# Hybrid decoder trunk on one core: VectorE merges the plain and the shared sums of a block pair, and an order is fixed between one step's last low part and the next step's first difference

## The chip, the cores and the metric

The kernel runs on one core of a Trainium2 chip. The metric is the device time of one execution in microseconds (us), given as the median of several runs. Beside it stands one profiled execution of the kernel, whose trace the views below come from. The engines are TensorE (PE in the views, with PEld for its weight loads), VectorE (DVE), ScalarE (ACT), GpSimd (POOL) and SyncE (SP); SP and POOL issue the transfers.

## The reference

One layer of a decoder trunk over 272 rows (16 meta tokens and 256 tokens) of 2048 float32 numbers: a combined projection, retention heads beside mLSTM heads, an output projection, and then a gated feed-forward part. Only the last part bears on the change:

```python
u = rmsnorm(h, norm_ffn)
up = causal_dwconv(u @ w_up, ffn_conv_w, ffn_conv_b)
gate, val = jnp.split(up, [FFN_DIM], axis=-1)          # FFN_DIM = 5632
h = h + (jax.nn.silu(gate) * val) @ w_down             # (256, 5632) @ (5632, 2048)
...
h = rmsnorm(h, norm_final)                             # meta rows are dropped
```

## The kernel before

**Numbers in two parts.** All products run in a 32-bit form of TensorE with fewer bits than float32. So each operand is split into a high part (a cast by ScalarE, tiles `whi`) and a low part (operand minus high part, by VectorE, tiles `wlo`), and three products are summed: high by high, high by low, low by high. For weights of a plain step this is `load_w` (lines 113 to 122): SP loads `wraw` (line 116), ScalarE casts (119), VectorE subtracts (121). `wraw` has four buffers, `whi` and `wlo` five each.

**Stages.** Input projection and heads, output projection (`in_wo`), then the feed-forward part in two halves of 22 tiles of 128 hidden columns each: in each half the up projection (`in_wu`), the convolution and the gate, and then the down projection (`in_wd`). The trace has the down projection of the first half from about 718 to 831 us, that of the second half from about 1083 to 1196 us.

**The down projection.** The output is 256 rows (two row tiles, `tt`) by 2048 columns (four blocks of 512, `b`). It is worked through in two pairs of blocks, `b` = 0 and then `b` = 2 (line 915). Each pair has 11 steps `q` over pairs of hidden tiles. Steps 0, 4, 9 and 10 are plain: four direct products (two row tiles, two blocks), into four PSUM banks `cs[tt, j]` (tiles `atps`, line 828). Steps 1, 2, 3, 5, 6, 7 and 8 are fast (`FAST`, function `seven`): the 2x2 block product is made with seven products instead of eight. Three of the seven go straight into the banks `cs`; the other four go into four shared banks `ps` (tiles `mmps`), whose sums and differences are wanted by several blocks. The last pair of the second half (`final`) takes the steps in another order, with two of the fast ones done plainly.

**A fast step** (`seven`, lines 830 to 869): SP loads the four weight tiles into one of two homes `left[turn]` (tile `hT`, lines 838 and 839; the first of them was made earlier and kept in DRAM). VectorE makes three differences of them: two at once into `ta` (line 842) and one into `tb` (line 843), which are buffers of `wraw`. Four groups are then split in turn by ScalarE and VectorE (lines 764 and 766): two from `hT`, then `ta`, then `tb`. TensorE takes the high parts (857, 858) and the low parts (860). A buffer of `wraw` comes free for SP's next load when the low part made from it is done.

**The end of a pair** (the border). After the last fast step, `share` (lines 878 to 894) empties the four shared banks: ScalarE copies `p1` into `x1` (882), VectorE makes `x6`, `x7`, the second `x6` and `x5` (884, 885, 887, 893), and each of the four is added onto its block of the result `hn` by an accumulating transfer of POOL (`onto`, line 876). After the last plain step the four banks `cs` are copied by ScalarE (line 949) into `x` tiles, and each is added onto its block by another accumulating transfer. A block thus gets two accumulating transfers at a border. There are three such borders: after the pairs 0 and 2 of the first half and after pair 0 of the second; the final pair is finished by VectorE in line 898. The first split of the next pair is placed behind the last copy of the border (`emptied`, line 854).

**What sets the order.** Each engine takes its own queue strictly in order. The order within a queue is chosen when the kernel is built, from the program's order and an estimate of when each instruction could run; `tc.issue_after(ins)` puts the instructions in its block behind `ins` where they are on the engine of `ins`. It makes no wait between engines.

Of the kernel before, what the change touches and what calls it, by code (L numbers as in the profile page):

```python
# [10 lines left out]
F32 = mybir.dt.float32  # L11
F32R = mybir.dt.float32r
AF = mybir.ActivationFunctionType
ALU = mybir.AluOpType
PSUM = bass.MemoryType.PSUM

P = 128
# [66 lines left out]
def trunk(ctx: ExitStack, tc: tile.TileContext, io, out: bass.AP):  # L84
    nc = tc.nc
# [120 lines left out]
    with pool("sq", 1, side="right") as sqp:  # L206
        for k0, k1 in [(0, 1), (1, 2)] + [(k, k + 2) for k in range(2, KT, 2)]:
            n = k1 - k0
# [3 lines left out]
            raw = wpool.tile([P, 2, W0], F32, name="wraw", bufs=4)[:, :n, :]  # L212
# [5 lines left out]
            for k in range(k0, k1):  # L218
                nc.scalar.activation(xh[:, k, :], hT[:, k, :], AF.Copy, scale=pcol("gmix", k))
                nc.vector.scalar_tensor_tensor(out=xl[:, k, :], in0=hT[:, k, :], scalar=pcol("gmix", k),  # L220
                                               in1=xh[:, k, :].bitcast(F32), op0=ALU.mult, op1=ALU.subtract)

            hi = wpool.tile([P, 2, W0 + GW], F32R, name="whi", bufs=5)[:, :n, :]
            lo = wpool.tile([P, 2, 2 * P], F32R, name="wlo", bufs=5)[:, :n, :]
            for i in ((slice(0, 1), slice(1, 2)) if k0 == 2 else (slice(0, n),)):
                copied = nc.scalar.copy(hi[:, i, 0:W0], raw[:, i])
                nc.vector.tensor_tensor(out=lo[:, i], in0=raw[:, i, 0 : 2 * P], in1=hi[:, i, 0 : 2 * P].bitcast(F32), op=ALU.subtract)
                parted = nc.vector.tensor_tensor(out=hi[:, i, W0:], in0=raw[:, i, 2 * P :], in1=hi[:, i, 2 * P : W0].bitcast(F32), op=ALU.subtract)
            for k in range(k0, k1):
                i = k - k0  # L230
                first, last = k == 0, k == KT - 1
                for j, (ps, t0) in enumerate(((k_ps, 0), (q_ps, TQ))):
                    w = hi[:, :, j * P : (j + 1) * P], lo[:, :, j * P : (j + 1) * P]
# [428 lines left out]
    midp_cm = pool("midp", 1, side="left")  # L662
    midp = midp_cm.__enter__()
    ss4 = midp.tile([P, 2, 5], F32, name="ss4")
    x5 = midp.tile([P, 5, 512], F32, name="x5")
    pace = midp.tile([P, 1], F32, name="pace")

    def x_tile(i):
        return x5[:, i, :]
# [74 lines left out]
    for half in range(2):  # L744
# [18 lines left out]
        def split(hi, lo, x, after=None):  # L763
            copied = nc.scalar.copy(hi, x)  # L764
            with tc.issue_after(after.ins) if after else nullcontext():
                return copied, nc.vector.tensor_tensor(out=lo, in0=x, in1=hi.bitcast(F32), op=ALU.subtract)  # L766
# [44 lines left out]
        if half == 1:  # L811
            table("natural_log_exp_and_others", copied)

        def product(ps, tt, q, w, first=False, last=False, c0=0, n0=0, n1=6, seed=False, seeded=False):

            hi, lo = w
            rows = slice(tt * P, (tt + 1) * P)
            cols = slice(c0, c0 + ps.shape[1])
            if q in PLAIN:
                k = 2 * PLAIN.index(q)  # L820
                ah, al = ([m[:, k + i, rows] for i in range(2)] for m in (mh, ml))
            else:
                f = FAST.index(q)
                ah, al = ([m[:, f, A12 if i else A11, :] if tt == 0 else m[:, f, A22, :] if i else a[:, BOTH.index(q), :] for i in range(2)]
                          for m, a in zip((sh, sl), a21))
            parts = [(a[i], hi, i) for i in range(2) for a in (ah, al)] + [(ah[i], lo, i) for i in range(2)]
            for n, (a, m, i) in list(enumerate(parts))[n0:n1]:
                nc.tensor.matmul(ps, a, m[:, i, cols], start=first and n == 0, stop=seed or last and n == 5, skip_group_check=seeded)  # L828

        def seven(b, q, cs, ps, first, last, after, norm):  # L830


            nonlocal turn
            f = FAST.index(q)
            raw = left[turn]
            turn = 1 - turn

            nc.sync.dma_start(raw[:, 0, :], early[b, q])
            nc.sync.dma_start(raw[:, 1:4, :], io["wd7"][b // 2, half * NQD + q][:, 1:4, :])
            ta, tb = (wpool.tile([P, 2, 512], F32, name="wraw", bufs=4) for _ in range(2))  # L840

            nc.vector.tensor_tensor(out=ta, in0=raw[:, 0:1, :].to_broadcast([P, 2, 512]), in1=raw[:, 1:3, :], op=ALU.subtract)
            nc.vector.tensor_tensor(out=tb[:, 0, :], in0=raw[:, 3, :], in1=raw[:, 0, :], op=ALU.subtract)
            copied = None
            for w, to in (
                (raw[:, 2:4, :], ((S4, cs[0, 1], False, False), (A12, cs[0, 0], False, False))),
                (raw[:, 0:2, :], ((S2, ps[2], first, last), (A11, ps[0], first, last))),
                (ta, ((S3, ps[1], first, last), (S1, ps[3], first, last))),
                (tb[:, 0:1, :], ((A22, cs[1, 0], False, False),)),
            ):  # L850
                hi = wpool.tile([P, 2, 512], F32R, name="whi", bufs=5)
                lo = wpool.tile([P, 2, 512], F32R, name="wlo", bufs=5)
                n = len(to)
                with tc.issue_after(after.ins) if first and after else nullcontext():
                    copied, _ = split(hi[:, :n, :], lo[:, :n, :], w)
                for i, (m, o, begin, _) in enumerate(to):
                    nc.tensor.matmul(o, sh[:, f, m, :], hi[:, i, :], start=begin, stop=False)  # L857
                    nc.tensor.matmul(o, sl[:, f, m, :], hi[:, i, :], start=False, stop=False)  # L858
                for i, (m, o, _, end) in enumerate(to):
                    nc.tensor.matmul(o, sh[:, f, m, :], lo[:, i, :], start=False, stop=end)  # L860
            if norm:

                with tc.issue_after(copied.ins):
                    for g in norm:
                        squares(*g)
                reached = nc.gpsimd.tensor_tensor(out=junk[:, 0:1], in0=tb[:, 0, 0:1], in1=tb[:, 0, 0:1], op=ALU.add)
                with tc.issue_after(reached.ins):
                    for tt, _, c0, c1 in norm:
                        times_gain(tt, c0, c1)
# [4 lines left out]
        def onto(tt, b, x):  # L874

            nc.gpsimd.dma_start(block(tt, b), x, accum_op=ALU.add)  # L876

        def share(ps, b, final):

            p1, p7, p6, p5 = ps  # L880
            x6, x7, x5, x1 = (x_tile(i) for i in range(4))
            nc.scalar.copy(x1, p1)  # L882
            onto(0, b, x1)
            nc.vector.tensor_tensor(out=x6, in0=p6, in1=x1, op=ALU.add)
            nc.vector.tensor_tensor(out=x7, in0=p7, in1=x6, op=ALU.add)
            onto(1, b, x7)
            nc.vector.tensor_tensor(out=x6, in0=x6, in1=p5, op=ALU.subtract)
            if final:

                nc.vector.tensor_tensor(out=block(0, b + 1), in0=block(0, b + 1), in1=x6, op=ALU.add)  # L890
            else:
                onto(0, b + 1, x6)
            nc.vector.tensor_tensor(out=x5, in0=x7, in1=p5, op=ALU.subtract)
            onto(1, b + 1, x5)

        def add(ps, tt, c0):
            h = hn[:, tt, c0 : c0 + ps.shape[1]]
# [17 lines left out]
        for b in (0, 2):  # L915
            cs = {}
            for j in range(2):
                for tt in range(2):
                    cs[tt, j] = at.tile([P, 512], F32, name="atps")
            ps = [mm.tile([P, 512], F32, name="mmps") for _ in range(4)]  # L920

            final = half == 1 and b == 2
            steps = [0, 1, 4, 2, 7, 3, 5, 6, 8, 9, 10] if final else range(NQD)
            fast = [q for q in steps if q in FAST and not (final and q in BOTH)]
            plain = [q for q in steps if q not in fast]
            alone = plain[-lag:] if final else []
            for q in steps:
                if q in fast:
                    due = []
                    if final and q != fast[0]:  # L930
                        due, gains = gains[:1], gains[1:]
                    seven(b, q, cs, ps, q == fast[0], q == fast[-1], emptied, due)
                    if q == fast[-1]:
                        with tc.high_priority() if final else nullcontext():
                            share(ps, b, final)
                    continue
                for j in range(2):
                    if j == 1 and q in alone:
                        continue
                    w = load_step(b + j, q)  # L940
                    for tt in range(2):
                        product(cs[tt, j], tt, q, w, q == plain[0], q == plain[-1 - (lag if final and (tt, j) == (1, 1) else 0)])
            for j in range(2):
                for n, tt in enumerate(range(2)):
                    c = (b + j) * 512
                    if not final:

                        x = x_tile((4, 3, 1, 0)[2 * j + n])
                        emptied = nc.scalar.copy(x, cs[tt, j])
                        onto(tt, b + j, x)  # L950
                        if half == 1:
                            gains.append((tt, b + j, c, c + 512))
                    elif j == 0:
                        add(cs[tt, j], tt, c)
                        squares(tt, b, c, c + 512)
                        times_gain(tt, c, c + 512)
# [116 lines left out]
```

## Time and profile before

| | us |
|---|---|
| median of 3 runs (lowest to highest) | 1206.83 (1206.01 to 1209.47) |
| the profiled execution's own time | 1206.01 |
| its span in the trace | 1204.2 |
| TensorE busy | 1194.5 |
| VectorE busy | 971.1 |
| ScalarE busy | 708.1 |
| GpSimd busy | 167.3 |

The rest of the profiled execution's time, 1.8 us, lies around the span. Busy time is a sum over the whole span; an engine that is busy for less than the span can still be the one that others wait for in one stage. The transfers of the program move 263.27 MB.

### The profile page before, as it was taken

How to read it: one execution, taken by the hardware profiler on the slowest of the kernel's cores; microseconds unless marked ns; L12 is line 12 of the kernel's file. 1: busy time of each engine (PE TensorE's matmuls, PEld its weight loads, DVE VectorE, ACT ScalarE, POOL GpSimd, SP SyncE). 2: the span in 40 equal slices, each digit the busy share in tenths (PEclk: the TensorE clock that was granted, in tenths of full speed). 3: DMA queues.
4: the chain of work that ended last, by engine and by line, in shares of the span. 5: the costliest groups of instructions: out<-in, count | busy, mean ns of one | idle time of the engine just before them, and what ended most of it. 6: DMA issues, size and time to landing. Idle time of an engine off the chain costs nothing.

```text
span 1204.2 us, 22798 instructions
## 1 busy us (share of the span) xinstructions
PE 1194.5 (99%) x8956; PEld 1151.2 (96%) x8956; DVE 971.1 (81%) x1446; ACT 708.1 (59%) x964; POOL 167.3 (14%) x222
## 2 busy tenths in 40 slices
PE   9999999999999999999999999999999999999997
PEld 9999999999999999999999998878999999998886
DVE  8967778766775966788888889997697878789897
ACT  8747746655656656555555556665554655556664
POOL 0100001111110311021112100202023112100232
PEclk9999999999999999999999999999999999999999
DMA  8865565566565965766866744949777767755956
GB/s 280 275 208 162 169 187 169 197 182 192 171 189 168 345 204 176 252 219 203 263 217 212 225 178 175 272 182 272 279 249 250 234 247 242 253 184 211 281 170 200
DMA packets 83005, 263.27 MB, mean 219 GB/s; under 512 B 14673, under 2 KB 18897, under 8 KB 82769
## 3 DMA queue, kind: packets, MB, share of 16 engines
q1 hardware_dynamic: 71952, 223.85, 56.9%
q0 software_dynamic: 10368, 37.11, 10.1%
q8 instruction: 70, 1.15, 0.4%
q10 hardware_dynamic: 576, 0.85, 0.2%
q14 instruction: 39, 0.31, 0.1%
HBM read 243.42 MB, written 11.27 MB: 211 GB/s over the span
## 4 chain that ended last, share of the span: by engine, by line
PE 97%; DMA 1%; DVE 1%; ACT 0%; issue 0%; SPq 0%; DVEq 0%; ACTq 0%
PE mmps L128 26%; PE mmps L129 25%; PE mmps L131 25%; PE atps L828 8%; PE mmps L860 2%; PE mmps L857 2%; PE mmps L858 2%; PE atps L858 1%; PE atps L857 1%; PE atps L860 1%; PE atps L380 1%; DMA wraw<-in_wd 1%; PE atps L372 0%; DMA hT<-in_xT 0%; PE atps L128 0%; PE atps L131 0%
## 5 line engine op out<-in xcount | busy, mean ns | idle before, releaser
L119 ACT CAST whi<-wraw 128x1024 fp32r<-128x1024 f32 x352 | 368.5, 1049 | 311.0 <-PE mmps L129 200.9
L121 DVE TENSOR_TENSOR wlo<-wraw,whi 128x1024 fp32r<-128x1024 f32 x352 | 432.5, 1231 | 68.9 <-ACT whi L119 66.7
L128 PE MATMUL mmps<-uh,whi 128*128 128x258 f32 x1408 | 346.1, 283 | 0.0
L129 PE MATMUL mmps<-ul,whi 128*128 128x258 f32 x1408 | 346.0, 283 | 0.0
L128 PEld LDWEIGHTS mmps<-uh,whi 128*128 128x128 f32 x1408 | 267.6, 190 | 0.1
L129 PEld LDWEIGHTS mmps<-ul,whi 128*128 128x128 f32 x1408 | 267.1, 190 | 0.1
L128 PE MATMUL mmps<-xh,whi 128*128 128x272 f32 (+2 forms) x864 | 219.8, 288 | 0.0
L129 PE MATMUL mmps<-xl,whi 128*128 128x272 f32 (+2 forms) x864 | 218.3, 286 | 0.0
L131 PE MATMUL mmps<-uh,wlo 128*128 128x258 f32 x1408 | 196.5, 282 | 0.0
L131 PEld LDWEIGHTS mmps<-uh,wlo 128*128 128x128 f32 x1408 | 179.9, 189 | 0.0
L129 PEld LDWEIGHTS mmps<-xl,whi 128*128 128x128 f32 x864 | 162.9, 189 | 0.0
L128 PEld LDWEIGHTS mmps<-xh,whi 128*128 128x128 f32 x864 | 162.5, 188 | 0.1
L131 PE MATMUL mmps<-xh,wlo 128*128 128x272 f32 (+2 forms) x864 | 126.6, 285 | 0.0
L131 PEld LDWEIGHTS mmps<-xh,wlo 128*128 128x128 f32 x864 | 114.2, 188 | 0.0
L764 ACT CAST whi<-hT 128x1024 fp32r<-128x1024 f32 x52 | 53.6, 1052 | 26.5 <-PE atps L828 7.9
L681 DVE TENSOR_TENSOR cu<-mmps,rstd 128x258 f32<-128x258 f32 x88 | 37.3, 424 | 38.1 <-PE mmps L131 37.5
L766 DVE TENSOR_TENSOR wlo<-hT,whi 128x1024 fp32r<-128x1024 f32 x52 | 62.2, 1221 | 5.9 <-ACT whi L764 4.7
L129 PE MATMUL mmps<-mixl,whi 128*128 128x258 f32 x256 | 63.0, 283 | 0.0
L128 PE MATMUL mmps<-mixh,whi 128*128 128x258 f32 x256 | 62.4, 282 | 0.0
L766 DVE TENSOR_TENSOR wlo<-wraw,whi 128x1024 fp32r<-128x1024 f32 (+1 forms) x52 | 52.2, 1038 | 0.9 <-PE mmps L860 0.2
L764 ACT CAST whi<-wraw 128x1024 fp32r<-128x1024 f32 (+1 forms) x52 | 43.0, 837 | 16.5 <-PE mmps L858 7.1
L876 POOL DMA_DIRECT2D hn<-x x27 | 23.6, 1033 | 202.6 <-ACT x L882 174.8
(284 smaller groups left out, 1732.9 us busy)
## 6 DMA issues: line engine op xcount, KB each, us to landing
wraw<-in_wu SPq DMA_DIRECT2D x176, 512.0 KB, 4.5
wraw<-in_wi SPq DMA_DIRECT2D x108, 512.0 KB, 4.1
hT<-in_wd SPq DMA_DIRECT2D x26, 768.0 KB, 4.6
wraw<-in_wd SPq DMA_DIRECT2D x36, 512.0 KB, 4.9
wraw<-in_wo SPq DMA_DIRECT2D x32, 512.0 KB, 4.1
x<-in_wd POOLq DMA_DIRECT2D x13, 768.0 KB, 7.5
hn<-x POOLq DMA_DIRECT2D x27, 256.0 KB, 7.9
hT<-kept SPq DMA_DIRECT2D x26, 256.0 KB, 2.8
```

The source lines that it names most:

```text
L119: nc.scalar.copy(hi, raw)
L121: nc.vector.tensor_tensor(out=lo, in0=raw, in1=hi.bitcast(F32), op=ALU.subtract)
L128: nc.tensor.matmul(ps, hi[:, k, :], xh(kk), start=kk == first, stop=False)
L129: nc.tensor.matmul(ps, hi[:, k, :], xl(kk), start=False, stop=False)
L131: nc.tensor.matmul(ps, lo[:, k, :], xh(kk), start=False, stop=kk == last)
L681: evacuated = nc.vector.tensor_tensor(out=u, in0=ps[:, :NQ], in1=rstd2, op=ALU.mult)
L764: copied = nc.scalar.copy(hi, x)
L766: return copied, nc.vector.tensor_tensor(out=lo, in0=x, in1=hi.bitcast(F32), op=ALU.subtract)
L828: nc.tensor.matmul(ps, a, m[:, i, cols], start=first and n == 0, stop=seed or last and n == 5, skip_group_check=seeded)
L857: nc.tensor.matmul(o, sh[:, f, m, :], hi[:, i, :], start=begin, stop=False)
L858: nc.tensor.matmul(o, sl[:, f, m, :], hi[:, i, :], start=False, stop=False)
L860: nc.tensor.matmul(o, sh[:, f, m, :], lo[:, i, :], start=False, stop=end)
```

## The change

Two edits. First, at the three borders the four results of `share` stay in their `x` tiles; when a bank `cs[tt, j]` is complete, VectorE adds the bank to the tile, and the sum goes onto the block with one accumulating transfer. ScalarE's four copies of line 949 and four of the eight transfers of a border are gone, and `x5` has four tiles instead of five. In the final pair the transfers of `x1` and `x7` stand behind the sum `x7` in the program's order. Second, in the first half's down projection, and there in steps 6, 7 and 8 of both pairs and in step 3 of the second, VectorE's difference `ta` is placed behind the last low part (that of `tb`) of the fast step before it.

```diff
-    x5 = midp.tile([P, 5, 512], F32, name="x5")
+    x5 = midp.tile([P, 4, 512], F32, name="x5")
...
         def seven(b, q, cs, ps, first, last, after, norm):
...
-            nc.vector.tensor_tensor(out=ta, in0=raw[:, 0:1, :].to_broadcast([P, 2, 512]), in1=raw[:, 1:3, :], op=ALU.subtract)
+            nonlocal parted7
+            with tc.issue_after(parted7.ins) if parted7 is not None and (half == 0 and (q > 5 or b == 2 and q == 3)) else nullcontext():
+                nc.vector.tensor_tensor(out=ta, in0=raw[:, 0:1, :].to_broadcast([P, 2, 512]), in1=raw[:, 1:3, :], op=ALU.subtract)
...
-                    copied, _ = split(hi[:, :n, :], lo[:, :n, :], w)
+                    copied, parted7 = split(hi[:, :n, :], lo[:, :n, :], w)
...
         def share(ps, b, final):
...
             nc.scalar.copy(x1, p1)
-            onto(0, b, x1)
             nc.vector.tensor_tensor(out=x6, in0=p6, in1=x1, op=ALU.add)
             nc.vector.tensor_tensor(out=x7, in0=p7, in1=x6, op=ALU.add)
-            onto(1, b, x7)
+            if final:
+                onto(0, b, x1)
+                onto(1, b, x7)
             nc.vector.tensor_tensor(out=x6, in0=x6, in1=p5, op=ALU.subtract)
...
-            else:
-                onto(0, b + 1, x6)
             nc.vector.tensor_tensor(out=x5, in0=x7, in1=p5, op=ALU.subtract)
-            onto(1, b + 1, x5)
+            if final:
+                onto(1, b + 1, x5)
+            return {(0, 0): x1, (1, 0): x7, (0, 1): x6, (1, 1): x5}
...
             for q in steps:
+                if q not in fast:
+                    parted7 = None
...
-                        x = x_tile((4, 3, 1, 0)[2 * j + n])
-                        emptied = nc.scalar.copy(x, cs[tt, j])
+                        x = shares[tt, j]
+                        emptied = nc.vector.tensor_tensor(out=x, in0=cs[tt, j], in1=x, op=ALU.add)
                         onto(tt, b + j, x)
```

More of the change, by code (lines that the diff above doesn't have):

```diff
@@ L927, in trunk @@
             for q in steps:
+                if q not in fast:
+                    parted7 = None
                 if q in fast:
@@ L934, in trunk @@
                         with tc.high_priority() if final else nullcontext():
-                            share(ps, b, final)
+                            shares = share(ps, b, final)
                     continue
```

## The prediction

> **What bounds the kernel now.** I read the page first, then the busy times by stretch, then the chain that ended last and the timeline of the engines around its breaks. The page:
>
> ```profile
> span 1204.2 us, 22798 instructions
> ...
> PE 1194.5 (99%) x8956; PEld 1151.2 (96%) x8956; DVE 971.1 (81%) x1446; ACT 708.1 (59%) x964; POOL 167.3 (14%) x222
> ...
> PE 97%; DMA 1%; DVE 1%; ACT 0%; issue 0%; SPq 0%; DVEq 0%; ACTq 0%
> ```
>
> TensorE is busy for all but 9.7 us of the span and carries 97% of the chain. The change takes no product away, so only TensorE's idle time can be won. The stretches of the two down projections (columns: stretch; its length; busy us of PE, PEld, DVE, ACT, POOL with counts; granted clock; DMA share; GB/s) say where that is:
>
> ```profile
> 718.00:762.00 44.00, 44.00 (x194) 36.09 (x193) 40.62 (x44) 27.69 (x31) 0.00 (x0) 1.00 0.57 207
> 762.00:780.00 18.00, 18.00 (x80) 14.80 (x79) 16.70 (x19) 11.63 (x16) 7.07 (x8) 1.00 1.04 250
> 780.00:832.00 52.00, 51.22 (x230) 41.68 (x230) 44.56 (x46) 30.05 (x34) 3.47 (x4) 1.00 0.66 216
> ...
> 1083.00:1130.00 47.00, 47.00 (x209) 38.64 (x208) 43.70 (x48) 30.70 (x35) 1.41 (x2) 1.00 0.66 237
> 1130.00:1147.00 17.00, 17.00 (x76) 13.93 (x75) 13.81 (x15) 12.01 (x15) 6.11 (x7) 1.00 1.05 259
> 1147.00:1204.00 57.00, 49.61 (x239) 41.12 (x237) 48.06 (x60) 31.04 (x49) 16.81 (x13) 0.96 0.57 185
> ```
>
> Up to 1147 us one row has a gap, 780 to 832: 52.00 - 51.22 = 0.78 us idle. The last row's 7.4 us are the final norm and the output's transfers, which the change does not touch. The second thing to see is VectorE: 40.62 of 44 and 16.70 of 18 us, with TensorE full. It runs close behind, and the change gives it work. The 0.78 us are two breaks of the chain that ended last:
>
> ```profile
> 786.95 1.15 DVE wlo L766
> 788.11 3.62 DMA wraw<-in_wd
> 791.83 1.06 ACT whi L119
> ...
> 810.77 1.06 DVE wraw L842
> 812.59 1.15 DVE wlo L766
> 813.75 3.41 DMA wraw<-in_wd
> 817.26 1.06 ACT whi L119
> ```
>
> Both times VectorE's low part releases a buffer, SP's load of a plain step's weights (step 4, then step 9, of the second pair) starts into it, ScalarE casts, and TensorE has waited. Its own timeline there:
>
> ```profile
> 791.94 0.62 PE L860 MATMUL mmps<-wlo,sh 128*128 128x512 f32 x2
> 792.93 0.51 PE L828 MATMUL atps<-whi,mh 128*128 128x512 f32 x1 [0.36 <-ACT whi L119]
> 793.27 0.40 PE L828 MATMUL atps<-whi,ml 128*128 128x512 f32 x1
> ...
> 817.32 0.63 PE L860 MATMUL mmps<-wlo,sh 128*128 128x512 f32 x2
> 818.36 0.50 PE L828 MATMUL atps<-whi,mh 128*128 128x512 f32 x1 [0.42 <-ACT whi L119]
> 818.70 0.40 PE L828 MATMUL atps<-whi,ml 128*128 128x512 f32 x1
> ```
>
> A lone product shows 0.39 us or a little more and two show 0.62, so starts are 0.23 apart when TensorE flows. At the first break the pair at 791.94 should be followed at 792.40, and is at 792.93: 0.53 lost; the next start is 0.34 on instead of 0.23: 0.11 more. At the second, 818.36 against 817.78 is 0.58, and again 0.11. Together **1.33 us**, the whole of what can be won in these stages.
>
> **The change part by part.** *The order of differences and low parts.* VectorE's queue at the two breaks:
>
> ```profile
> 781.23 1.23 DVE L766 TENSOR_TENSOR wlo<-hT,whi 128x1024 fp32r<-128x1024 f32 x1 [0.51 <-PE atps L860]
> 785.12 1.23 DVE L842 TENSOR_TENSOR wraw<-hT 128x1024 f32<-128x1024 f32 x1 [2.67 <-DMA hT<-in_wd]
> 786.26 0.68 DVE L843 TENSOR_TENSOR wraw<-hT 128x512 f32<-128x512 f32 x1
> 786.87 1.82 DVE L766 TENSOR_TENSOR wlo<-wraw,whi 128x1024 fp32r<-128x1024 f32 x2
> ...
> 808.50 2.36 DVE L766 TENSOR_TENSOR wlo<-hT,whi 128x1024 fp32r<-128x1024 f32 x2
> 810.77 1.22 DVE L842 TENSOR_TENSOR wraw<-hT 128x1024 f32<-128x1024 f32 x1
> 811.90 0.69 DVE L843 TENSOR_TENSOR wraw<-hT 128x512 f32<-128x512 f32 x1
> 812.50 1.82 DVE L766 TENSOR_TENSOR wlo<-wraw,whi 128x1024 fp32r<-128x1024 f32 x2
> ```
>
> At 785.12 step 3's difference has held up the queue for 2.67 us, waiting for its weights, while step 2's two low parts (786.87, for `ta` and `tb`) stood behind it. Those release the buffers that step 4's load wants. With the change they go first, at about 782.5 instead of 786.87, so the load can start at about 783.6 instead of 788.11, 4.5 us earlier against 0.64 us of stall. What comes later is step 3's difference, but only if its weights are there before 784.3 (782.5 + 1.82); they came at 785.1, so nothing is late. At 810.77 nothing waits: step 8's two differences (about 1.73 us, 810.77 to 812.50) simply change places with step 7's two low parts. The low part of `ta` then ends at about 811.95 instead of 813.7, and the load starts 1.7 us earlier against 0.69 us of stall. Late by 1.82 is step 8's difference, so its cast; behind it in VectorE's queue are step 8's low parts from `hT`, which keep their time, because the four instructions together are as long as before. SP's queue holds no new wait. The other five places (step 6 and 7 of the second pair, 6 to 8 of the first) lie where TensorE is full; they can win nothing there, and VectorE's sum is unchanged. I take the whole 1.33 as gain; the bounds are 0 and 1.33.
>
> *The border.* Four copies leave ScalarE, four adds come to VectorE:
>
> ```profile
> L949 ACT COPY x<-atps x8: 577/590/611, 772.2 to 833.4; 128x512 f32<-128x512 f32 x8
> L884 DVE TENSOR_TENSOR x<-mmps,x x2: 684/684/685, 763.4 to 820.9; 128x512 f32<-128x512 f32 x2
> ```
>
> The added instruction has the form of line 884: 0.684 us, four of them 2.74 us a border, 8.2 over three; ScalarE is spared 4 x 0.590 = 2.36 a border. [...]
>
> What covers the 2.74 us? Around the first and the third border:
>
> ```profile
> 772.33 1.23 DVE L121 TENSOR_TENSOR wlo<-wraw,whi 128x1024 fp32r<-128x1024 f32 x1 [0.28 <-ACT whi L119]
> ...
> 1138.13 1.23 DVE L121 TENSOR_TENSOR wlo<-wraw,whi 128x1024 fp32r<-128x1024 f32 x1 [0.60 <-ACT whi L119]
> 1141.02 2.36 DVE L766 TENSOR_TENSOR wlo<-hT,whi 128x1024 fp32r<-128x1024 f32 x2 [1.67 <-ACT whi L764]
> ```
>
> In the first half VectorE idles 0.28 at the border, 0.51 at 781.23 and 2.67 at 785.12: 3.46 us ahead of the first break, against 2.74. In the second half 0.60 + 1.67 = 2.27 right there, the 1.67 being a wait for a cast that stood behind ScalarE's four copies, which are gone. So the cover is 3.46 and about 2.3, and if it failed altogether each border would cost TensorE up to 2.74. The second border lies in front of the up projection, where the four banks `cs` are not wanted for 250 us; nothing there needs the adds soon.
>
> The banks of the next pair are the tighter point, since TensorE's next direct product overwrites them:
>
> ```profile
> 773.17 0.39 PE L828 MATMUL atps<-whi,mh 128*128 128x512 f32 x1
> ```
>
> This is its first; ScalarE had emptied the bank at 772.78 (772.2 + 0.58). An add placed behind the low part at 772.33 would end at about 774.2 and stall TensorE by 1.0 us; placed ahead of it, from 772.05 where VectorE falls idle (772.33 - 0.28), it ends at 772.7. The first split behind `emptied` now orders only low parts, so ScalarE's casts are freer. I take 0; the bounds are 0 and about 1 a border.
>
> *The transfers.* What the four fewer are worth:
>
> ```profile
> L876 POOL DMA_DIRECT2D hn<-x x27 | 23.6, 1033 | 202.6 <-ACT x L882 174.8 <-ACT x L949 17.5 <-DVE x L885 5.7
> ...
> q0 software_dynamic: 1152, 2.10, 27.5%
> ...
> 755.00:785.00 30.00, 30.00 (x133) 24.62 (x132) 25.28 (x26) 16.98 (x21) 7.07 (x8) 1.00 1.01 283
> ```
>
> From 755 to 785 us the DMA engines are full (share 1.01). Between 755 and 800, eight accumulating transfers of the border (1152 packets, 2.10 MB) take 27.5% of 45 us, 12.4 us of all 16 engines, 1.55 each. Four fewer give 6.2 us back in the stretch where step 3's weights came 2.67 us late. [...] None of this reaches TensorE by itself: it makes the cover of the border wider. In the final pair the two transfers keep their producers and POOL's queue; 0.
>
> **Sum.** Against the profiled execution: 1206.01 - 1.33 + 0 = 1204.7. The median of the three runs was 0.82 above that execution, so 1206.83 - 1.33 = **1205.5**. A measurement of this kernel can tell about 0.3% from no change, 3.6 us; this is a third of it.
>
> **The rivals.**
> *One stall stays or is replaced.* The adds use up the idle time ahead of the first break, and step 2's low parts come 2 us or more later than I think; or the first bank is emptied late (1.0 us, above). For it: VectorE at 16.70 of 18 us. Against: the relief of the transfers. It leaves the gain of the second break: 1206.83 - 0.69 = 1206.1. Chance 0.17.
> *Nothing changes.* The loads of steps 4 and 9 wait for something else as well, SP's own order or ScalarE's place in it, or the built order puts the low parts no earlier: 1206.8. Against it: the chain names the low part at both breaks. Chance 0.18.
> *Slower: VectorE becomes the bound behind the borders.* The adds are queued where they wait for TensorE's last product of the pair, with low parts behind them, and TensorE then runs out of low parts. Each border can cost the 2.74 us that come to VectorE. This decides once what the borders let through exceeds the 1.33 won; slower by 0.3% takes 3.62 + 1.33 = 4.95 of the 8.2 us. With all of it, 1206.83 + 8.2 - 1.33 = 1213.7. Against it: 3.46 and 2.27 us of cover. Chance 0.07.
> *Faster by over 0.3%.* It would need 3.6 us, and the rows show 1.33 of stall; only a new order of the last 57 us could give it. Chance 0.03.
>
> **How the numbers follow.** The forecast keeps 0.55. With "one stays" and "nothing", 0.90 lies within 0.3%; 0.07 slower, 0.03 faster. The range: the forecast's 1205.5, less the 0.82 by which a run can lie below the median and 0.5 for the order elsewhere, gives 1204.2; at the top 1206.8 of "nothing" plus the spread above the median (1209.47 - 1206.83 = 2.6) is 1209.4, which I cut to 1209.0.
>
> **What would show it.** Right: no wait of TensorE for line 119 near 793 and 818 us; row 780 to 832 full; step 2's two low parts ahead of step 3's difference; step 4's load issued near 784; line 876 with 15 transfers instead of 27; VectorE near 971.1 + 8.2 = 979.3, ScalarE near 708.1 - 12 x 0.59 = 701.0; DMA share below 1 from 762 to 780. Wrong: TensorE waiting for an add in front of its first product of a pair, or for low parts after a border; the two breaks still there.

## The result, and the profile after

| | before | after |
|---|---|---|
| median of 22 runs each (lowest to highest), us | 1207.7 (1205.33 to 1210.46) | 1205.76 (1204.68 to 1207.8) |
| ratio, 95% interval | | 0.9984 (0.9978 to 0.999) |
| the profiled execution's own time; its span, us | 1206.01; 1204.2 | 1206.42; 1204.5 |
| VectorE, ScalarE, GpSimd busy, us | 971.1, 708.1, 167.3 | 977.4, 704.3, 156.4 |
| software queue (accumulating transfers among it): packets | 10368 | 8640 |

The change is 1.9 us faster, 0.16%. The two profiled executions do not show it: their spans differ by 0.3 us the other way. How that fits is the main question below. Lines move by a few in the changed kernel: 828 becomes 830, 842 becomes 846, 857, 858 and 860 become 861, 862 and 864, 876 becomes 880, and the new add is line 956.

Busy times by stretch, the rows that answer to those of before (PE, PEld, DVE, ACT, POOL, clock, DMA share, GB/s):

```profile
718.00:762.00 44.00, 44.00 (x196) 36.15 (x195) 40.47 (x44) 28.21 (x32) 0.00 (x0) 1.00 0.60 207
762.00:780.00 18.00, 18.00 (x80) 14.79 (x79) 17.10 (x20) 9.41 (x11) 3.56 (x4) 1.00 0.63 184
780.00:832.00 52.00, 51.93 (x236) 42.65 (x234) 49.48 (x54) 31.73 (x35) 1.41 (x2) 1.00 0.66 223
...
1130.00:1147.00 17.00, 17.00 (x76) 13.96 (x75) 15.99 (x19) 10.60 (x11) 3.51 (x4) 1.00 0.79 216
```

TensorE's idle time between 780 and 832 us has fallen from 0.78 to 0.07. The DMA share at the two borders inside a half has fallen from 1.04 to 0.63 and from 1.05 to 0.79. VectorE is fuller, and in this trace TensorE never waits for its adds. VectorE's queue at the place of the first break:

```profile
775.69 1.28 DVE L956 TENSOR_TENSOR x<-atps,x 128x512 f32<-128x512 f32 x2
776.89 2.34 DVE L766 TENSOR_TENSOR wlo<-hT,whi 128x1024 fp32r<-128x1024 f32 x2
...
782.36 2.36 DVE L766 TENSOR_TENSOR wlo<-hT,whi 128x1024 fp32r<-128x1024 f32 x2 [0.79 <-PE atps L830]
784.64 1.82 DVE L766 TENSOR_TENSOR wlo<-wraw,whi 128x1024 fp32r<-128x1024 f32 x2
786.38 1.22 DVE L846 TENSOR_TENSOR wraw<-hT 128x1024 f32<-128x1024 f32 x1
```

Step 2's two low parts (784.64) now stand ahead of step 3's difference (786.38), and the 2.67 us of waiting for step 3's weights are gone. But the low parts end later than forecast, and what follows is not as quick. The chain that ended last, from there to the break and then in the final pair:

```profile
784.64 1.23 DVE wlo L766
785.89 6.23 DMA wraw<-in_wd
792.21 1.06 ACT whi L119
793.31 1.20 PE atps L830 x4
...
1179.96 1.24 DVE wlo L121
1181.22 6.85 DMA wraw<-in_wd
1188.09 1.06 ACT whi L119
```

Step 4's load started at 785.89 instead of 788.11, but took 6.23 us instead of 3.62. So 0.34 us of stall are left there (TensorE starts at 792.62, two products, then 793.31). The break at step 9 is gone. And another stands near the end: the last weights of the final pair took 6.85 us to land, and TensorE lost 0.53 us in front of and just behind 1189.19. One execution of each kernel is too little to say what the change does to a wait that hangs on landing times; hence the repeats.

### The profile page after: what moved, and what is told of

The parts are those of the page before. It is cut to its first block, busy times and chain, and to the rows that moved or that the text cites. A ratio compares the mean times of both kernels' runs of the same rounds, so it can differ in the third digit from the quotient of the medians.

```text
span 1204.5 us, 22769 instructions
## 1 busy us (share of the span) xinstructions
PE 1195.0 (99%) x8956; PEld 1152.0 (96%) x8956; DVE 977.4 (81%) x1458; ACT 704.3 (58%) x952; POOL 156.4 (13%) x210
## 3 DMA queue, kind: packets, MB, share of 16 engines
q0 software_dynamic: 8640, 33.96, 8.7%
## 4 chain that ended last, share of the span: by engine, by line
PE 96%; DMA 2%; DVE 1%; ACT 1%; issue 0%; SPq 0%; DVEq 0%; ACTq 0%
PE mmps L128 26%; PE mmps L129 25%; PE mmps L131 25%; PE atps L830 7%; PE mmps L862 2%; PE mmps L861 2%; PE mmps L864 2%; DMA wraw<-in_wd 1%; PE atps L862 1%; PE atps L861 1%; PE atps L864 1%; PE atps L380 1%; DVE wlo L766 0%; PE atps L372 0%; DMA wraw<-in_w 0%; PE atps L128 0%
## 5 line engine op out<-in xcount | busy, mean ns | idle before, releaser
L830 PE MATMUL atps<-whi,mh 128*128 128x512 f32 (+1 forms) x132 | 50.8, 386 | 0.3 <-ACT whi L119 0.3
```

## The experiments

Ratios are against runs of the kernel before on the same chip; that kernel's median lay between 1206.4 and 1208.4 us from one set of runs to the next, so only ratios and medians of one set are compared. Beside the time, each trace gives two lengths: D1, from the first product of the first half's down projection to the first of the next up projection, and D2, from the last product of that up projection to the last product of all. TensorE's work in D1 and in D2 is the same in all kernels, and the least seen (110.33 us in five traces, 112.88 in two) is taken as the length without a stall. The 254 us between them and the 7.9 us behind them were the same to 0.06 us everywhere; the start before D1 varied between 717.36 and 718.79 us with the first loads, in no order (TensorE's waits for what ScalarE makes of them, lines 219 and 226, came to 0 in four_transfers and to 1.5 us in order_step3).

| trace | D1 | D2 | lost over the least | ratio (interval) |
|---|---|---|---|---|
| before | 111.69 | 113.13 | 1.6 | |
| before_again | 113.11 | 114.72 | 4.6 | 1.0005 (0.9993 to 1.0016) |
| after | 110.69 | 113.74 | 1.2 | 0.9984 (0.9978 to 0.999) |
| after_again | 110.95 | 114.10 | 1.8 | 0.9982 (0.9973 to 0.999) |
| after_third | 110.87 | 112.88 | 0.5 | 0.9973 (0.9963 to 0.9982) |
| border_only | 110.33 | 113.15 | 0.3 | 0.9986 (0.9975 to 0.9996) |
| order_only | 110.33 | 115.22 | 2.3 | 0.998 (0.9971 to 0.999) |
| order_step3 | 110.33 | 113.40 | 0.5 | not timed |
| order_678 | 110.33 | 115.86 | 3.0 | not timed |
| scalar_order | 111.47 | 114.32 | 2.6 | 1.0002 (0.9994 to 1.0011) |
| four_transfers | 110.33 | 112.88 | 0.0 | 0.9989 (0.998 to 0.9998) |
| border_eight | 120.48 | 113.88 | 11.2 | 1.0078 (1.0064 to 1.0092) |
| border_own_last | 110.40 | 112.98 | 0.2 | 0.9988 (0.9979 to 0.9996) |
| border_own_again | 110.63 | 113.10 | 0.5 | 0.9978 (0.9968 to 0.9988) |

**The kernel before, again (before_again).** No edit.

> The kernel before, unchanged, as a measure of how far two runs of one program differ. Ratio 1.000 by every theory. Its trace: if the stalls of the first trace (0.64 us at step 4 and 0.69 us at step 9 of the second pair in the first half) are set by the order of VectorE's queue alone, they come back within 0.2 us each. If they hang on how long loads take to land, they differ by more than that, and a stall can stand at another load.

The same program lost 4.6 us where it had lost 1.6. The two breaks came back, 0.78 and 0.90 us instead of 0.64 and 0.69. New ones, 0.49 and 0.64 us, stand at both borders inside a half, where TensorE wants the first bank of the next pair. What it waited for (who, for whom; us in total, times, longest):

```profile
PE atps L828 <- ACT whi L119: 1.7, 3, 0.6
...
PE atps L828 <- ACT x L949: 0.6, 2, 0.4
```

Line 949 is the copy that empties the bank. ScalarE's queue at the second half's border shows why it was late:

```profile
1139.54 1.05 ACT L119 CAST whi<-wraw 128x1024 fp32r<-128x1024 f32 x1 [1.56 <-DMA wraw<-in_wd]
1140.50 2.04 ACT L949 COPY x<-atps 128x512 f32<-128x512 f32 x4
```

The four copies stand behind a cast of the next pair's weights, which waits for its load. In the trace of the prediction the first border's copy of that bank ended 0.39 us ahead of TensorE's need (772.78 against 773.17), so this wait could not be seen there. The change takes these copies off ScalarE's queue; in their place TensorE can come to wait for an add (below).

**The changed kernel, again (after_again, after_third).** No edit.

> The changed kernel, unchanged. About 1.9 us under the kernel before. In its first trace TensorE lost 0.34 us at step 4 of the second pair and 0.65 us at the final pair's last weight load. Theory A (order): the loss at step 4 comes back, since the adds put the low parts 2 us later than without them. Theory B (landing times): it is 0 to 1 us here, and the loss in the final pair, whose load took 6.85 us, is gone.

> The changed kernel once more, on the chip of the next one. 1.5 to 2 us under before. From the two traces: 0.3 to 0.6 us of stall in the first half's down projection, 0.7 to 1 us at the final pair's last load.

Lost: 1.2, 1.8 and 0.5 us in three traces, against 1.6 and 4.6 of before. The means, 1.2 and 3.1, differ by 1.9 us, as the medians do; with two and three traces that is agreement, not proof. The stall at step 4 was 0.34, 0.28 and 0.10 us. The stall near the end was 0.6, 1.0 and 0 us. The three traces are of one program with one order, so it points to landing times (6.85 us for the last weights in the first trace); before had it too (0.85 us in its second trace, where that load took 6.70 us). It is not always the last load: in the second trace the last weights took 4.89 us and were cast at once (1186.12), but an earlier load took 5.71 us instead of 4.03, VectorE's queue ran about 1 us late from there, and TensorE waited for low parts. So the theory of the order (A) and that of the landing times (B) both missed a part: the stall at step 4 came back smaller, and the one near the end was there in the second trace and not in the third.

At the first border the third trace lost 0.43 us in front of the next pair's first product, the second and the first none:

```profile
773.35 1.28 DVE L956 TENSOR_TENSOR x<-atps,x 128x512 f32<-128x512 f32 x2
...
774.18 0.47 PE L830 MATMUL atps<-whi,mh 128*128 128x512 f32 x1 [0.19 <-ACT whi L764]
```

The row puts this down to a cast of step 1, which a direct product does not read. The first of the two adds, the one that empties this bank, ends at 774.04, and the product starts 0.14 us later. It started as long after the first add wherever it was late behind one: 0.15 us in border_own_again (773.47 and 773.62, 0.30 us lost), 0.14 at both borders of border_eight. So this is a wait for an add.

**One edit at a time (border_only, order_only).** The changed kernel without its second edit, and the kernel before with the second edit alone:

```diff
-            with tc.issue_after(parted7.ins) if parted7 is not None and (half == 0 and (q > 5 or b == 2 and q == 3)) else nullcontext():
+            with nullcontext():
                 nc.vector.tensor_tensor(out=ta, ...)
```

> VectorE's adds and the single transfer per block, with the difference not tied to the low part. Theory A (the order carries the gain, the border is covered): both stalls of before stay, 1.33 us, and the time is that of before, 0 to +1 us. Theory B (the removed transfers carry it, since loads land earlier and more evenly): 1 to 1.9 us under before, with the wait of the difference of step 3 for its weights (2.67 us) gone.

> The difference tied behind the low part, with ScalarE's copies and eight transfers at a border as before. Theory A: both stalls go, 1.3 us under before or a little more. Theory B: only the stall at step 9 goes (0.7 us), and runs differ as much as those of before (5 us from lowest to highest).

Each edit alone gives about what both give: 0.9986, 0.998 and 0.9982, with intervals that lie over one another. By these medians the gains do not add, though the intervals are nearly too wide to say so; D1 says it more plainly. Either edit alone brings it to its least, with both breaks of the first half gone. With the order edit alone eight transfers and ScalarE's copies are still there, and in this trace D2 is long, with 1.6 us lost at the second half's border:

```profile
1139.76 0.50 PE L830 MATMUL atps<-whi,mh 128*128 128x512 f32 x1 [1.34 <-ACT x L955]
```

Theory A, that the order carries the gain and the border only has to be covered, falls on border_only. It was expected to keep both breaks; it has neither. But its built order is not that of before (VectorE's low parts stand elsewhere), so it does not yet say whether the transfers did it.

**The transfers alone (four_transfers).** The kernel before, with the shared sums' transfers left out at the borders (the line shown, and the other three likewise):

```diff
             nc.scalar.copy(x1, p1)
-            onto(0, b, x1)
+            if final:
+                onto(0, b, x1)
...
```

> The kernel before with ScalarE's copies, but the four transfers of the shared sums are left out at the three borders, so the output lacks those sums. Theory T: loads at the border land earlier, no stall there, 1.5 to 2 us under before, as much as the border edit alone (2.2 us). Theory Q: a smaller part, since the copies still stand behind the cast, 0 to 1 us; and the stalls behind low parts at steps 4 and 9 of the second pair stay.

TensorE's order here is that of before, and in VectorE's queue step 3's difference still stands ahead of step 2's low parts:

```profile
782.57 1.23 DVE L842 TENSOR_TENSOR wraw<-hT 128x1024 f32<-128x1024 f32 x1 [0.30 <-DMA hT<-in_wd]
783.71 0.68 DVE L843 TENSOR_TENSOR wraw<-hT 128x512 f32<-128x512 f32 x1
784.31 1.82 DVE L766 TENSOR_TENSOR wlo<-wraw,whi 128x1024 fp32r<-128x1024 f32 x2
```

It waits 0.30 us for its weights instead of 2.67, the low parts come at 784.31 instead of 786.87, and both breaks are gone. There is no stall in the whole of D1 and D2. The DMA share from 755 to 785 us is 0.81 instead of 1.01. Step 3's own weights (0.79 MB) were issued at 777.54 instead of 778.09 and landed after 4.90 us instead of 6.91. The other traces agree: this load, issued between 777 and 781 us, took 5.88 to 7.18 us in the five traces with eight transfers at that border, and 4.90 to 5.34 in the seven with four. (Left out are the two with eight whose order had moved: scalar_order issued it at 781.45, when all eight but one had landed, and it took 4.32 us; in border_eight everything lies some 5 us later.) So the transfers are enough of a cause by themselves: they make step 3's weights late, that holds up VectorE's queue, and both breaks are what is left of it some 8 and 33 us later. The gain in the median is 1.3 us by the ratio, with an interval of 0.2 to 2.4; theory T had 1.5 to 2, and theory Q had both breaks stay, which they did not.

**Each place of the order edit (order_step3, order_678).** The kernel before with the condition cut to `b == 2 and q == 3`, and to `q > 5`.

> The kernel before with the order edit at one place only: step 3 of the second pair, first half. Theory A (each place cures its own stall): the stall at step 4 (0.64 us before) is gone, the one at step 9 (0.69) stays. Theory L (one lateness: step 3's weights come late, VectorE idles 2.67 us, and both stalls are what is left of that): both are gone, since VectorE gets those 1.8 us of low parts done in the wait and stays ahead to step 9.

> The kernel before with the order edit at steps 6, 7 and 8 only. Theory A: the stall at step 9 is gone, the one at step 4 stays, about 0.6 us. Theory L: the same, since the places lie behind the late weights; VectorE still idles 2 to 3 us ahead of step 3's difference.

With step 3 alone the stall at step 9 is gone as well: theory L (one lateness, two breaks) holds there. With steps 6 to 8 alone the stall at step 4 was gone too, which neither theory had: VectorE waited 1.64 us for step 3's weights instead of 2.67, and step 4's load, at 787.30 instead of 788.11, was in time. The stall at step 4 is small beside the spread of that wait. One execution each, so no more can be read from them. The wait for line 955 at the second half's border was there again in order_678 (1.8 us lost), and not in order_step3.

**The copies moved in ScalarE's queue (scalar_order).** The kernel before, with the cast of the next pair's second weights behind the copies:

```diff
-                    w = load_step(b + j, q)
+                    with tc.issue_after(emptied.ins) if emptied and (q, j) == (0, 1) else nullcontext():
+                        w = load_step(b + j, q)
```

> The kernel before, but the cast and the low part of a pair's second block in step 0 are placed behind the four bank copies of the border; eight transfers as before. Theory Q (ScalarE's queue: the copies stand behind a cast that waits for its load): TensorE's wait for line 949 (now 950) at the borders, 0.6 us in the second trace of before and 1.3 us with the order edit alone, is gone; the two breaks behind low parts stay unless the built order moves; about 1 us under before. Theory T (the eight transfers make every load late, whatever stands behind it): the wait moves to the cast that now comes later, and the time is that of before.

No wait for the copies is left, but the time is that of before. The trace lost 1.04 us ahead of the border, at step 9 of the first pair, waiting for a cast whose weights were late, with a DMA share of 1.07 from 762 to 780 us. Both breaks were gone here too, with all eight transfers: the built order had moved, and one of step 2's two low parts stood ahead of step 3's difference. Theory Q (ScalarE's queue) names a real wait, yet this kernel gains nothing that the runs can tell.

**Eight transfers with VectorE's adds (border_eight).** border_only with four transfers of zeros added at each border.

```diff
+    none = midp.tile([P, 512], F32, name="none")
+    nc.vector.memset(none, 0.0)
...
+            if not final:
+                onto(0, b, none)
...
+            else:
+                for tt, i in ((1, b), (0, b + 1), (1, b + 1)):
+                    onto(tt, i, none)
```

> The border edit alone, with four more accumulating transfers at each border that add a tile of zeros to the four blocks where the kernel before added the shared sums: eight transfers again, but the banks are emptied by VectorE. Theory T: the gain is lost, about 1207.6, with the difference of step 3 waiting 2 us or more for its weights. Theory Q: the gain stays, about 1205.5, no wait of TensorE at a pair's first products.

It does not settle the question. It is 9.4 us slower by the ratio, but 4.2 us of its stalls lie in the first pair, ahead of any border transfer: the built order came out differently from there on, with steps of the convolution between VectorE's low parts. The transfers of zeros, too, were queued among and behind the real ones (782.05 us and later), not at the place of the shared sums. That adds on VectorE stay harmless under eight transfers was therefore not shown. Two things can be read in it. TensorE lost 2.6 us at 800.83 behind a load that took 8.88 us while those transfers were still landing. And its list of waits names the add, which is line 963 here, at both borders inside a half:

```profile
PE atps L832 <- DVE x L963: 0.5, 2, 0.3
```

**The last weights in a buffer of their own (border_own_last, border_own_again).** border_only, and in the final pair:

```diff
-                ws[q] = load_step(3, q, more if n % 2 else wpool)
+                ws[q] = load_step(3, q, more if n % 2 else wpool, more if n == 3 else None)
```

where the new argument gives the loaded weights a tile of their own in the pool `more`.

> The border edit alone, and the final pair's last weights are loaded into a buffer of their own instead of one that a low part has to release. In the traces so far that last load cost TensorE 0.0, 0.8, 0.6, 0.9, 0.4 and 0.1 us near the end of the products. If the wait for the released buffer is its cause, no such stall, and 0.5 us less than the border edit alone in the median (about 1205.0). If the load is late for another reason (its place in SP's queue), the stall stays.

> The border edit alone with a buffer of its own for the last weights, once more, against the changed kernel on the same chip. Both lost pieces of the changed kernel are gone in its first trace (0.07 and 0.11 us of stall left), so it should be 0.5 to 1.3 us faster than the changed kernel. If the medians agree within 0.3 us, the stalls in single traces do not stand for the mean of many runs.

The last load no longer stalls TensorE (0.1 and 0.2 us are left around it). Yet on one chip the medians are 1205.44 against 1205.1 of the changed kernel: the expected 0.5 to 1.3 us did not come, and a stall in a single trace did not stand for the mean of many runs. The changed kernel's trace of that set had no such stall either. No version here that computes the whole result beats the changed kernel.

## Why the prediction came out as it did

- **The sum.** Forecast 1205.5, measured 1205.76; forecast gain 1.33, measured 1.9 (0.1 to 0.22%). Sign and size hold, and time within 0.3% of before. That the two times lie 0.26 us apart is in part luck: the forecast started from a median of three runs, 1206.83, where 22 runs gave 1207.7, and that 0.87 us is nearly offset by the 0.6 us by which the gain was put too low.
- **The two breaks.** Right that they would go and that late low parts were their last link. The break at step 9 went entirely; the one at step 4 from 0.64 to 0.34, 0.28 and 0.10. The step that failed there: the low parts come "at about 782.5", the load "at about 783.6". They came at 784.64 and the load at 785.89, since the adds, ahead of them in the queue, moved the low parts of step 1 from 775.32 to 776.89 and VectorE then waited 0.79 us for a buffer. And the load took 6.23 us, started 0.8 us behind step 5's megabyte; the prediction had let it keep its 3.62 us.
- **Who carries it.** "I take the whole 1.33 as gain" of the order edit, and of the transfers "none of this reaches TensorE by itself". The second is wrong: four_transfers clears both breaks with the order of before. One lateness can be cured at its source (fewer transfers) or hidden (low parts first), and the gains of the two edits overlap.
- **What was not in the forecast.** The borders were priced for a loss only. They had stalls of their own in other executions of before (0.5 and 0.6 us in before_again, 1.6 in order_only), and the trace read for the prediction was of an execution with none: 1206.01 us, near the low end of 1205.33 to 1210.46. The gain is larger than that trace could show. How much of the 1.9 us comes from the borders and how much from the two breaks is not shown.
- **The cover.** Taken as 0 a border, with a bound of about 1 us. It held in the first two traces of the changed kernel, and the third border's idle time came free with ScalarE's copies. It did not hold in the third, which lost 0.43 us at the first border waiting for an add in front of the next pair's first product. That is a sign which the prediction had named as one of being wrong; it stayed inside the bound. The step that failed is the time of the add, forecast to end at about 772.7: in the same order as in the first trace, where it ended at 772.90, VectorE's queue ran 1.1 us late behind a load that took 6.96 us instead of 6.04, and the add ended at 774.04.
- **The prices.** The add took 0.680 (forecast 0.684):

```profile
L956 DVE TENSOR_TENSOR x<-atps,x x8: 676/680/683, 772.2 to 832.8; 128x512 f32<-128x512 f32 x8
...
q0 software_dynamic: 576, 1.05, 14.8%
```

With one operand from PSUM it is no slower than line 843's 0.68 from SBUF alone. The second row is the software queue from 755 to 800 us: 14.8% of 45 us is 6.7, against 12.4 before, so 5.7 us of all engines were given back, forecast 6.2. VectorE's busy time rose by 6.3 instead of 8.2 and ScalarE's fell by 3.8 instead of 7.1. Part of that is that neighbours overlap in the records (two adds show 1.28, four copies 2.14); the rest is left open, as nothing waits on it.
- **The rivals.** "Slower" has no sign in any time but that of border_eight, whose order differs; the waits for an add cost up to 0.43 us in a trace of the changed kernel. "One stall stays" came true in a small way, for step 4.

## What to carry to other kernels

When an engine's queue stands still for late data, as VectorE's did here for 2.67 us with two low parts behind it, ask both what makes the data late and what could be done meanwhile: here either cured it, and the two gains were nearly one gain (0.9986 and 0.998 alone, 0.9982 together). Where a stall hangs on a transfer's landing, one trace shows one draw (0.34, 0.28 and 0.10 us at step 4 in three traces of one program); profile the unchanged kernel twice before counting what can be won. An edit that changes the number of instructions can change the whole built order, so read the queues before reading the time.

## What the runs showed of the hardware

- The same program lost 1.6 and 4.6 us in two executions, most of it to waits that hang on when loads landed (1.33 and 3.66 us). Runs of the kernel before spread over 5.1 us, those of the changed kernel over 3.1.
- An accumulating transfer of 0.26 MB inside SBUF took 1.55 us of all 16 DMA engines where a border had eight of them (27.5% of 45 us), and 1.66 us where it had four (14.8%).
- With those engines at a share of 1.01 from 755 to 785 us, weights of 0.79 MB landed after 6.91 us and held up VectorE for 2.67; with four transfers fewer and step 3's difference still ahead of step 2's low parts (four_transfers, share 0.81), after 4.90 us, and for 0.30.
